# Narrower score matmuls in a dilated attention: 128 key columns in place of 256 for blocks that see one block of keys

## The chip, the cores and the metric

The kernel runs on one core of a Trainium2 chip. The metric is the device time of one execution in microseconds; the time before is the median of three runs. A profile of one further execution gives every instruction's start and duration. The engines are named PE (matmul), PEld (its weight load, which runs beside PE), DVE, ACT, POOL and SP (which issues DMAs).

## The reference

One layer of a decoder: RMSNorm, one input projection, two mixers side by side (a gated linear attention, "GLA", and a dilated sliding-window attention), an output projection, an MLP with squared ReLU, and a final norm. There are 2048 tokens of width 1024, and everything is in float32. The change lies in the dilated attention: 8 heads of width 64, three branches with (window, dilation) of (128, 1), (512, 4) and (2048, 16). In each branch the tokens are sorted by their residue modulo the dilation, and cut into blocks of 128:

```python
qb = to_sub(q).reshape(B, dilation, H, nb, L, Dh)     # L = 128
kb = band(to_sub(k))                                  # a block and the one before it
s = jnp.einsum('bdhcqe,bdhcke->bdhcqk', qb, kb).astype(f32) + bias[:, None]
s = jnp.where(mask, s, NEG)
m = jnp.max(s, axis=-1, keepdims=True)
p = jnp.exp(s - m)
den = jnp.sum(p, axis=-1, keepdims=True)
o = jnp.einsum('bdhcqk,bdhcke->bdhcqe', p, vb.astype(f32)) / den
```

A query block sees its own block of keys and the one before it. The first block of each residue has none before it. With 2048 tokens that is 1 block of 16 for dilation 1, 4 of 16 for dilation 4, and all 16 for dilation 16, where each residue has one block only.

## The kernel before

**Stages.** The kernel has four stages on PE: the input projection (to about 524 us of the profile), the attention together with the GLA (524 to about 862), the output projection, and the two MLP products (to the end). The projections and the MLP are computed as sums of products of the type `float32r` (FR in the code), a float32 whose low mantissa bits are rounded away: each operand is split into a high and a low part, and `mm3` (L141 to L144) adds three products. The attention's scores use the same type: the head dimension of 64 is doubled to 128 rows of the array, high and low parts of the queries against the high part of the keys at L852 (`k1`) and against the low part at L854 (`k2`). Transposes, value products and the GLA are in plain float32.

**Blocks and units.** For each head and branch there are 16 query blocks n. A `Unit` is 2 blocks (branches 0 and 1) or 4 blocks (branch 2). `Unit.scores` takes them in pairs; a pair shares one bank of PSUM (`ps_c`), 256 columns for each block. `windows(br, n)` says from which block of keys on the scores are computed (`first`) and which of the two blocks that follow are used (`used`). A block with two blocks of keys uses both. A block with one is computed for 256 columns too, and half of them are left aside: in branches 0 and 1 the second half, which is the next block; in branch 2 the second half, which is the next residue, but for n = 15, which starts at residue 14 and uses the second half. `k_cols` cuts the 256 columns out of the keys: contiguous in branch 0, with stride 4 in branch 1 (32 x 8 columns of one residue), and 2 x 16 x 8 columns of two neighbouring residues in branch 2.

**What follows the scores.** DVE adds the bias to the used columns and reduces each row (L864), ACT takes the exponential (L865). `Unit.transpose` turns each used 128x128 block on PE (L874) and copies four of them at a time to SBUF (L881 on ACT or L883 on DVE). `Unit.values` multiplies each with 65 columns of values (L893), and DVE takes four blocks from PSUM (L896).

**What sets the order.** The loop at L1186 writes, for each k, the scores of unit k + 3, the transposes of unit k and the values of unit k - 2 alternately, with a step of the GLA (`gla_steps`) after most units, and other work by a plan in units (`at_unit`): packing of queries on POOL (`pack_q`, L806), combining of the branches (`combine`, L921), loads by SP. From L731 on this program order isn't binding: the program is built with `schedule_with_timeline_sim=True`, so a planner with its own prices for instructions places them on the engines' queues, apart from those that the code pins with `keep_in_program_order`. The GLA step has a round trip: L1020 on PE, L1021 on ACT, L1023 and L1026 on POOL, L1033 on PE.

Of the kernel before, what the change touches and what calls it, by code (L numbers as in the profile page):

```python
# [116 lines left out]
def emit(tc, a, stop=99):  # L117
    nc = tc.nc
    V, A, G, T, SP = nc.vector, nc.scalar, nc.gpsimd, nc.tensor, nc.sync
# [6 lines left out]
    def ps(tag):  # L126
        return psum.tile([128, 512], F32, name="ps_" + tag, tag=tag, bufs=BANKS[tag])
# [5 lines left out]
    def view(t, shape):  # L133
        n = int(np.prod(shape))
        names = "abcd"[:len(shape)]
        return t[:, :n].rearrange(f"p ({' '.join(names)}) -> p {' '.join(names)}", **dict(zip(names, shape)))
# [475 lines left out]
    with tc.manual_schedule(engines={nc.tensor.engine, nc.vector.engine, nc.scalar.engine, nc.gpsimd.engine}):  # L612
# [22 lines left out]
        w = view(first_w[0][0], (2, 4, 256))  # L635
# [172 lines left out]
    def windows(br, n):  # L808

        step = (1, 4, 1)[br]  # L810
        if br == 2:
            return (n, [0]) if n < 15 else (n - 1, [1])
        return (n, [0]) if n < step else (n - step, [0, 1])

    def k_cols(t, br, first):
        if br == 0:
            return t[:, 128 * first:128 * first + 256]
        if br == 1:
            b, r = divmod(first, 4)
            return t.rearrange("p (x r i) -> p r x i", r=4, i=8)[:, r, 16 * b:16 * b + 32, :]  # L820
        return t.rearrange("p (x r i) -> p r x i", r=16, i=8)[:, first:first + 2]

    turn = [0]
    ring = {}
# [1 line left out]
    def work(name):  # L826
        i = ring.get(name, 0)
        ring[name] = (i + 1) % 4
        return ring[name + "s"][:, i]

    class Unit:
# [6 lines left out]
        def scores(self):  # L838

            br, h = self.b.br, self.b.h  # L840
            qs, k1, k2 = self.b.head
            qs = packed.get((h, br), qs)
            O = self.b.O
            pe = work("pe")
            each = 2 if br < 2 else 1
            for at in range(0, len(self.ns), 2):
                sp = ps("c")
                rest = []
                for e, n in enumerate(self.ns[at:at + 2]):
                    first, used = windows(br, n)  # L850
                    q, s = qs[:, 128 * n:128 * n + 128], sp[:, 256 * e:256 * e + 256]
                    T.matmul(s, q, k_cols(k1, br, first), start=True, stop=False)  # L852
                    yield
                    T.matmul(s, q, k_cols(k2, br, first), start=False, stop=True)  # L854
                    w = 128 * len(used)
                    s = s[:, 128 * used[0]:128 * used[0] + w]
                    p = pe[:, 128 * each * (at + e):128 * each * (at + e) + w]
                    rest.append((n, s, p, w, used, first))
                    if e == 0:
                        yield  # L860
                for n, s, p, w, used, first in rest:
                    bias = nb[br][:, h, :] if w == 256 or br == 2 else nb[br][:, h, 128:]
                    nm = O[:, n, 130 + h % 2:131 + h % 2]
                    V.tensor_tensor_reduce(p, s, bias, scale=1.0, scalar=BIG, op0=OP.add, op1=OP.min, accum_out=nm)  # L864
                    A.activation(p, p, AF.Exp, bias=nm, scale=-1.0)  # L865
                    for i, u in enumerate(used):
                        self.blocks.append((p[:, 128 * i:128 * i + 128], n,
                                            first + ((1, 4, 1)[br] if br < 2 else 1) * u, u == used[0], u == used[-1]))
                yield
# [283 lines left out]
    for pr in range(4):  # L1153
# [3 lines left out]
        for hh, br in seq:  # L1157
            b = Branch()
            b.h, b.br = 2 * pr + hh, br
            m = 4 if br == 2 else 2  # L1160
            first = len(units)
# [238 lines left out]
    for at, t in enumerate(tiles):  # L1400
# [8 lines left out]
        p = [ps("a"), ps("a")]  # L1409
# [179 lines left out]
    first, parts_at = 7 * (NP - 1), {}  # L1589
# [9 lines left out]
    for at in range(7, len(jobs1)):  # L1599
# [10 lines left out]
        n = at + 6 - len(jobs1)  # L1610
# [15 lines left out]
    for ph, (_, chained, _, _) in enumerate(PRODUCTS):  # L1626
# [3 lines left out]
        for k in range(4):  # L1630
            n = 4 * ph + k
# [74 lines left out]
```

## Time and profile before

| | |
|---|---|
| median of 3 runs | 2267.77 us (2267.43 to 2269.95) |
| the profiled execution | 2271.47 us |
| its span from first to last instruction | 2269.7 us |
| mean granted clock of TensorE | 0.998 |
| L852, L854: matmuls of scores | 384 rows each |
| L874: transposes | 600 rows |
| L893: value products | 1200 rows |

In views of groups a row reads: line, engine, operation, output and inputs, shapes, count, busy time in us, mean ns of one, idle time before them and what ended it. In a timeline a row reads: start and length in us, engine, line, operation, operands, count of merged instructions. In a view by stretches a row reads: the stretch, its length, then busy us and count of each engine, the granted clock, the share of DMA and GB/s. Rows of waits read: who waited for whom, us in total, times, the longest in us. PE's matmuls overlap in the records, so distances between starts say what one costs, and durations do not.

### The profile page before, as it was taken

The page shows a single profiled execution, that of the slowest core. Times are in us where ns is not written, and L with a number is a line of the kernel's source. Part 1 is how long each engine was busy: PE and PEld are TensorE (multiplying, and loading weights), DVE is VectorE, ACT ScalarE, POOL GpSimd, SP SyncE. Part 2 cuts the span into 40 slices and gives each one's busy share as a digit, 9 for nine tenths or more (in the row PEclk, how much of TensorE's full clock was granted, in tenths as well). Part 3 has the DMA queues.
Part 4 walks back from the last instruction along what each step waited for, and adds up shares of the span by engine and source line. Part 5 has one row for each costly group of instructions (what it writes and reads, how often), then busy time and mean ns, then how long its engine had stood idle before and what let it go on. Part 6 is the DMA issues. An engine that isn't in the chain of part 4 may idle for free.

```text
span 2269.7 us, 35245 instructions
## 1 busy us (share of the span) xinstructions
PE 2242.1 (99%) x12508; PEld 1941.8 (86%) x12508; DVE 1632.6 (72%) x3092; ACT 1219.0 (54%) x2421; POOL 481.5 (21%) x455
## 2 busy tenths in 40 slices
PE   9999999999999999999999999999999999999998
PEld 8978998799999998888788887888878888888877
DVE  7788778766667676445867678767776696566798
ACT  6665446535777784324655557555555533333446
POOL 1110002025285673000000000000006322032462
PEclk9999999999999999999999999999999999999999
DMA  5458754787668864678645456454479997677775
GB/s 199 138 175 241 250 166 123 221 249 231 197 210 245 262 199 158 208 229 270 216 128 165 128 165 212 153 177 151 140 241 278 312 320 259 207 249 256 259 257 190
DMA packets 361441, 478.59 MB, mean 211 GB/s; under 512 B 19958, under 2 KB 269319, under 8 KB 350129
## 3 DMA queue, kind: packets, MB, share of 16 engines
q1 hardware_dynamic: 356766, 467.69, 63.7%
q0 software_dynamic: 4352, 8.39, 2.0%
q8 instruction: 98, 1.61, 0.3%
q14 instruction: 79, 0.64, 0.1%
q10 hardware_dynamic: 146, 0.27, 0.0%
HBM read 326.54 MB, written 154.44 MB: 212 GB/s over the span
## 4 chain that ended last, share of the span: by engine, by line
PE 90%; DMA 3%; DVE 2%; issue 2%; POOL 1%; ACT 1%; POOLq 0%; SPq 0%; DVEq 0%; ACTq 0%
PE ps_a L143 10%; PE ps_a L142 10%; PE ps_a L144 10%; PE ps_c L143 8%; PE ps_c L142 8%; PE ps_c L144 8%; PE ps_a L893 4%; PE ps_d L143 4%; PE ps_o L144 4%; PE ps_d L144 4%; PE ps_o L143 4%; PE ps_o L142 4%; PE ps_d L142 4%; PE ps_d L874 3%; PE ps_c L852 2%; PE ps_c L854 2%
## 5 line engine op out<-in xcount | busy, mean ns | idle before, releaser
L1500 POOL TENSOR_TENSOR bs<-bs,rb 128x1024 f32<-128x1024 f32 x60 | 179.1, 2993 | 1069.9 <-DVE ca L487 836.2
L486 ACT ACTIVATE cb<-bs 128x1024 fp32r<-128x1024 f32 x104 | 110.3, 1061 | 287.7 <-issue 144.0
L487 DVE TENSOR_TENSOR cb<-bs,cb 128x1024 fp32r<-128x1024 f32 x104 | 161.1, 1549 | 139.6 <-ACT cb L486 139.6
L487 DVE TENSOR_TENSOR w1comb<-w1raw,w1comb 128x512 fp32r<-128x512 f32 x224 | 153.3, 686 | 90.6 <-ACT w1comb L486 90.0
L865 ACT ACTIVATE pe<-pe,O 128x256 f32<-128x256 f32 (+1 forms) x384 | 156.5, 453 | 45.8 <-DVE O L864 42.3
L893 PE MATMUL ps_a<-v,pt 128*128 128x65 f32 x1200 | 178.5, 253 | 2.5 <-ACT pt L881 1.9
L486 ACT ACTIVATE w1comb<-w1raw 128x512 fp32r<-128x512 f32 x224 | 139.4, 626 | 75.6 <-PE ps_c L144 26.7
L893 PEld LDWEIGHTS ps_a<-v,pt 128*128 128x128 f32 x1200 | 175.3, 195 | 3.5 <-ACT pt L881 2.1
L874 PE MATMUL ps_d<-ident,pe 128*128 128x128 f32 x600 | 159.4, 279 | 0.0
L864 DVE CUSTOM_DVE_ANT_0 pe<-ps_c,nb 128x256 f32<-128x256 f32 (+1 forms) x384 | 126.3, 360 | 40.9 <-PE ps_d L874 18.1
L286 ACT ACTIVATE wcomb<-wraw 128x512 fp32r<-128x512 f32 (+2 forms) x119 | 90.0, 757 | 98.7 <-PE ps_a L143 31.3
L142 PE MATMUL ps_c<-hb,w1comb 128*128 128x512 f32 x336 | 130.8, 389 | 0.5 <-ACT xs L1371 0.5
L143 PE MATMUL ps_c<-hb,w1comb 128*128 128x512 f32 x336 | 130.7, 389 | 0.0
L144 PE MATMUL ps_c<-hb,w1comb 128*128 128x512 f32 x336 | 130.5, 389 | 0.0
L487 DVE TENSOR_TENSOR ca<-ra,ca 128x1024 fp32r<-128x1024 f32 x84 | 121.8, 1451 | 0.1
L144 PE MATMUL ps_c<-cb,ca 128*128 128x512 f32 x312 | 121.4, 389 | 0.0
L143 PE MATMUL ps_c<-cb,ca 128*128 128x512 f32 x312 | 121.4, 389 | 0.0
L142 PE MATMUL ps_c<-cb,ca 128*128 128x512 f32 x312 | 121.4, 389 | 0.0
L1362 ACT ACTIVATE acc<-acc 128x512 f32<-128x512 f32 x96 | 60.7, 632 | 93.8 <-DVE acc L1377 40.4
L874 PEld LDWEIGHTS ps_d<-ident,pe 128*128 128x128 f32 x600 | 110.0, 187 | 0.1
L351 POOL TENSOR_TENSOR acc<-acc,misc 128x264 f32<-128x264 f32 (+1 forms) x32 | 39.2, 1237 | 313.4 <-DVE acc L350 287.0
L142 PE MATMUL ps_a<-wo,mT 128*128 128x512 f32 x256 | 101.3, 396 | 0.0
(411 smaller groups left out, 7111.4 us busy)
## 6 DMA issues: line engine op xcount, KB each, us to landing
ra<-actD SPq DMA_DIRECT2D x52, 1024.0 KB, 7.5
actD<-ring SPq DMA_DIRECT2D x176, 256.0 KB, 2.9
rb<-w_ff SPq DMA_DIRECT2D x88, 512.0 KB, 6.0
bs<-w_ff SPq DMA_DIRECT2D x72, 512.0 KB, 5.6
w1raw<-w_ff SPq DMA_DIRECT2D x64, 512.0 KB, 4.2
k<-kD SPq DMA_DIRECT2D x16, 1024.0 KB, 8.3
wraw<-w_in SPq DMA_DIRECT2D x48, 256.0 KB, 3.4
cmb<-boD SPq DMA_DIRECT2D x16, 528.0 KB, 7.6
```

What stands on the lines that cost most here:

```text
L142: T.matmul(out, sh, mh, start=first, stop=False, **kw)
L143: T.matmul(out, sl, mh, start=False, stop=False, **kw)
L144: T.matmul(out, sh, ml, start=False, stop=last, **kw)
L286: A.activation(hi, src, AF.Copy, scale=sc)
L486: A.activation(hi, src, AF.Copy)
L487: V.tensor_tensor(lo, src, hi.bitcast(F32), op=OP.subtract)
L864: V.tensor_tensor_reduce(p, s, bias, scale=1.0, scalar=BIG, op0=OP.add, op1=OP.min, accum_out=nm)
L865: A.activation(p, p, AF.Exp, bias=nm, scale=-1.0)
L874: T.transpose(pb[:, i * 128:i * 128 + 128], src, ident)
L893: T.matmul(self.b.opsum[:, n % 4], self.pt[:, i * 128:i * 128 + 128], self.b.v[:, blk, cols], start=first, stop=last)
L1362: A.activation(v, v, AF.Relu)
L1500: (engines or ((G,), (V, V))[len(sums) - 1])[e].tensor_tensor(v, v, r, op=OP.add if op == "+" else OP.subtract)
```

## The change

Score matmuls are computed for as many columns as there are blocks of keys in `used`: 128 or 256. In branch 2 `first` is always n and the keys of one residue are taken, 16 x 8 columns. The used part of a block's scores now always begins at the block's first column of PSUM, so the offset by `used[0]` goes away. The reduction, the exponential, the transposes and the value products keep their shapes.

```diff
         step = (1, 4, 1)[br]
         if br == 2:
-            return (n, [0]) if n < 15 else (n - 1, [1])
+            return n, [0]
         return (n, [0]) if n < step else (n - step, [0, 1])
 
-    def k_cols(t, br, first):
+    def k_cols(t, br, first, n):
         if br == 0:
-            return t[:, 128 * first:128 * first + 256]
+            return t[:, 128 * first:128 * first + 128 * n]
         if br == 1:
             b, r = divmod(first, 4)
-            return t.rearrange("p (x r i) -> p r x i", r=4, i=8)[:, r, 16 * b:16 * b + 32, :]
-        return t.rearrange("p (x r i) -> p r x i", r=16, i=8)[:, first:first + 2]
+            return t.rearrange("p (x r i) -> p r x i", r=4, i=8)[:, r, 16 * b:16 * b + 16 * n, :]
+        return t.rearrange("p (x r i) -> p r x i", r=16, i=8)[:, first]
...
                     first, used = windows(br, n)
-                    q, s = qs[:, 128 * n:128 * n + 128], sp[:, 256 * e:256 * e + 256]
-                    T.matmul(s, q, k_cols(k1, br, first), start=True, stop=False)
+                    w = 128 * len(used)
+                    q, s = qs[:, 128 * n:128 * n + 128], sp[:, 256 * e:256 * e + w]
+                    T.matmul(s, q, k_cols(k1, br, first, len(used)), start=True, stop=False)
                     yield
-                    T.matmul(s, q, k_cols(k2, br, first), start=False, stop=True)
-                    w = 128 * len(used)
-                    s = s[:, 128 * used[0]:128 * used[0] + w]
+                    T.matmul(s, q, k_cols(k2, br, first, len(used)), start=False, stop=True)
```

## The prediction

> **What bounds the kernel now.** I read the page first: the busy shares, then the chain that ended last.
>
> ```profile
> span 2269.7 us, 35245 instructions
> ...
> PE 2242.1 (99%) x12508; PEld 1941.8 (86%) x12508; DVE 1632.6 (72%) x3092; ACT 1219.0 (54%) x2421; POOL 481.5 (21%) x455
> ...
> PE 90%; DMA 3%; DVE 2%; issue 2%; POOL 1%; ACT 1%; POOLq 0%; SPq 0%; DVEq 0%; ACTq 0%
> ```
>
> PE is busy for 99% of the span and is 90% of the chain. The change touches two matmul lines, L852 and L854, which run only in the attention stage, from 524 to about 862 us. So the second view is the busy time by stretches of that stage, and the third PE's waits in it.
>
> ```profile
> core 0: us, PE busy (x) PEld busy (x) DVE busy (x) ACT busy (x) POOL busy (x), PEclk, DMA share, GB/s
> ...
> 600.00:700.00 100.00, 100.00 (x894) 98.90 (x894) 68.57 (x307) 77.46 (x234) 57.65 (x83) 1.00 0.70 215
> 700.00:800.00 100.00, 100.00 (x901) 98.90 (x901) 70.45 (x302) 79.44 (x243) 69.26 (x100) 1.00 0.85 263
> ```
>
> ```profile
> PE ps_o L1033 <- POOL gla L1023: 2.0, 1, 2.0
> PE ps_a L893 <- ACT pt L881: 1.9, 1, 1.9
> PE ps_c L852 <- DVE O L864: 0.8, 1, 0.8
> ```
>
> Between 600 and 800 us PE never pauses, and PEld, the weight load, is busy 98.9%. PE waits 4.7 us in the whole stage. ACT is the next engine, with a fifth of its time free. What a matmul takes from PE there is therefore end-to-end time, one for one, up or down. But two things are full, the array and the weight load, so the question is which of them a narrower matmul meets. Matmul durations in the trace overlap, so I use distances between starts.
>
> **How many matmuls change.** The scores of a block with one block of keys go through the 128-column form of the row reduction at L864:
>
> ```profile
> L864 DVE CUSTOM_DVE_ANT_0 pe<-ps_c,nb 128x128 f32<-128x128 f32 x168 | 40.8, 285 | 8.4 <-PE ps_d L874 1.7 <-PE ps_c L854 1.5 <-ACT gla L1064 1.3
> ```
>
> 168 blocks, each with one L852 and one L854, are 336 matmuls. From `windows`: per head 16 blocks of branch 2, 4 of branch 1 and 1 of branch 0; times 8 heads that is 128 + 32 + 8 = 168. So 256 of the matmuls are of branch 2 and 80 of the others.
>
> **What one costs now.** Three stretches in which scores follow scores, in branch 2, 1 and 0 in this order:
>
> ```profile
> 560.48 0.30 PE L852 MATMUL ps_c<-k,qp 128*128 128x256 f32 x1
> 560.61 0.30 PE L854 MATMUL ps_c<-k,qp 128*128 128x256 f32 x1
> ...
> 561.81 0.34 PE L893 MATMUL ps_a<-v,pt 128*128 128x65 f32 x2
> ```
>
> ```profile
> 574.68 0.28 PE L854 MATMUL ps_c<-k,qp 128*128 128x256 f32 x1
> ...
> 575.27 0.28 PE L852 MATMUL ps_c<-k,qp 128*128 128x256 f32 x1
> ```
>
> ```profile
> 594.24 0.28 PE L854 MATMUL ps_c<-k,qs 128*128 128x256 f32 x1
> ...
> 594.83 0.28 PE L852 MATMUL ps_c<-k,qs 128*128 128x256 f32 x1
> ```
>
> Branch 2: 10 starts from 560.48 to 561.81, 1.33 us, 133 ns each. Branches 1 and 0: 5 starts in 0.59 us each, 118 ns. Branch 2 reads keys 16 apart for two neighbouring residues, and pays 15 ns more for the same 256 columns.
>
> **What one costs after: the floor of the weight load.** No matmul of this rounded 4-byte kind (FR in the code) is narrower than 256 columns in the trace, so the price has to be bounded. Each score matmul loads its own 128 columns of weights (the queries), the second of a pair the same ones again. The nearest row for a matmul with little array work and a fresh load is a run of value products:
>
> ```profile
> 870.62 1.00 PE L893 MATMUL ps_a<-v,pt 128*128 128x65 f32 x8
> 871.46 0.49 PE L510 MATMUL ps_d<-ident,mx 128*128 128x128 f32 x3
> ```
>
> Eight records with only 65 columns take 0.84 us, 105 ns each, while the load of each is as large as that of a score. The cheapest mixture is the cycle of one transpose and two value records, where the loads come closest together:
>
> ```profile
> 561.99 0.28 PE L874 MATMUL ps_d<-ident,pe 128*128 128x128 f32 x1
> 562.10 0.33 PE L893 MATMUL ps_a<-v,pt 128*128 128x65 f32 x2
> ...
> 562.56 0.28 PE L874 MATMUL ps_d<-ident,pe 128*128 128x128 f32 x1
> ```
>
> The next transpose is at 562.27 and the one after at 562.56: 0.57 us for two cycles, 285 ns for three loads, 95 ns each. And plain 4-byte products of 128 columns:
>
> ```profile
> 577.99 0.39 PE L1053 MATMUL ps_o<-gla 128*128 128x128 f32 x2
> ...
> 579.33 0.27 PE L874 MATMUL ps_d<-ident,pe 128*128 128x128 f32 x1
> ```
>
> Twelve records (L1053 and L1054 in turn, two each) in 1.34 us: 112 ns each. So a record that loads 128 fresh columns takes 95 to 112 ns whatever it multiplies. I take **110 ns**, near the upper end, since scores mostly follow scores and not the cheap transposes.
>
> The Trainium skill ("TensorE: Matmul & The Clock Gate", section "LDWEIGHTS (loading the stationary operand)") reckons a weight load in ns as its columns divided by 1.2: 106.7 for 128. The 105 and 112 ns above agree with it, and the sum below by that figure would be 7.6 us.
>
> **The sum.** Branch 2: 256 x (133 - 110) = 5.9 us. Branches 1 and 0: 80 x (118 - 110) = 0.6 us. Together 6.5 us less on PE. With 112 it is 5.4 + 0.5 = 5.9 us, with 95 it is 9.7 + 1.8 = 11.5 us. If the narrow form keeps today's distances it is 0.
>
> **What else moves.** Nothing on DVE, ACT or POOL: the reduction, the exponential, the transposes and the value products have the shapes of before. The score block of n = 15 in branch 2 now lies in the first half of its 256 columns of PSUM and not in the second. No DMA and no wait is added; the keys are read in half the columns. Instruction order in this stage is set by a planner with its own prices for matmuls, which may exchange neighbours on PE. That I cost at nothing, because each record is near the floor whatever stands beside it; its bounds are the 4.7 us of waits that it could win and as much that it could add. The POOL chain (combining of branches, then L1026) on which PE waits at the end of the stage starts from PE:
>
> ```profile
> 831.61 1.13 PE L1033 MATMUL ps_o<-gla 128*128 128x256 f32 x4 [2.04 <-POOL gla L1023]
> ```
>
> By then nearly all changed blocks are done, so the chain and the PE work before it move together, and the wait stays 2 us. Cover for ACT: 6.5 us off 338 raises its share from 79% to 81%, so it doesn't become the bound.
>
> The profiled execution was 2271.47 us (span 2269.7 and 1.8 around it), 3.7 above the median of 2267.77. I take the 6 us off the median: **2262 us**, 0.3% less.
>
> **Rivals.**
>
> *The narrow form loses the fast rate (slower).* The fast rate is shown only from 256 columns up; no row says that it holds below. Plain 4-byte products are issued as two records each:
>
> ```profile
> L893 PE MATMUL ps_a<-v,pt 128*128 128x65 f32 x1200 | 178.5, 253 | 2.5 <-ACT pt L881 1.9
> ...
> L874 PE MATMUL ps_d<-ident,pe 128*128 128x128 f32 x600 | 159.4, 279 | 0.0
> ```
>
> (600 blocks of values, 1200 records). If a score matmul below 256 columns runs like those, it costs two records of 112 ns, 224 ns, in place of 133 or 118: 256 x 91 + 80 x 106 = 23.3 + 8.5 = 31.8 us more, 2299.6 us. The mechanism needs only that the width decides the mode, with the point somewhere between 128 and 256 columns. For it: the kinds share 4-byte operands and engine, and the gap in the evidence lies exactly there. Against it: the change alters no type, and a score matmul is one record today. The Trainium skill ("FP8 and Floating Point Precision", section "TensorE Precision Notes") says that true 4-byte products take four passes; the 112 ns records agree with two passes of 128 columns each, and the page is silent on narrow matmuls of the rounded kind.
>
> *The array alone sets the price (faster by more).* 512-column products of the rounded kind:
>
> ```profile
> 877.21 0.39 PE L143 MATMUL ps_a<-wo,mT 128*128 128x512 f32 x1
> ...
> 877.90 0.39 PE L143 MATMUL ps_a<-wo,mT 128*128 128x512 f32 x1
> ```
>
> Three in 0.69 us: 230 ns, against 118 for 256, thus 0.44 ns for a column; 128 columns would take 118 - 56 = 62 ns. Gain: 256 x 71 + 80 x 56 = 18.2 + 4.5 = 22.7 us, 2245 us. It needs loads of the rounded kind to be nearly twice as quick as those of the plain kind; the runs at 105 to 112 ns and PEld at 98.9% speak against it. The Trainium skill ("TensorE: Matmul & The Clock Gate", section "Back-to-back issue gap") gives N/2.4 + 2.5, that is 55.8 ns, for 128 columns, and about 81 ns where each matmul has its load; by 81 the gain would be 16.3 us. The run at 105 ns contradicts it for 4-byte weights.
>
> *Nothing is gained.* Distances stay at 118 to 133 ns because something other than the columns sets them (for branch 2 the load of the packed queries beside the strided keys), or the planner's new order gives the gain back: 2267.8 us. Against it: the difference between 118 and 133 goes with how the keys are read.
>
> **How the numbers follow.** Forecast 0.46, slower form 0.37, array alone 0.06, nothing gained 0.11. Below 0.2%, 4.5 us, this kernel's measurement can't tell a change from none. The forecast's own range, floors of 95 to 115 ns and some planner's noise, is 2255 to 2264; a fifth of it falls within 0.2%. Faster: 0.37 + 0.06 + a little of the last = 0.44; same 0.18; slower 0.38. To leave out no more than two in ten, the range must reach the slower form: 2254 to 2301. It leaves out the array alone and the dearest tenth of the slower form.
>
> **What would show it.** L852 and L854 split into 216 rows of 256 columns and 168 of 128 each. In branch 2, starts of neighbouring scores 105 to 115 ns apart show the floor of the load; about 224 ns, or two records for each narrow matmul, shows the lost rate; 62 the array. The rounds of L893 and L874 keep their 285 ns. I am wrong if the stage's length changes by other than 5 to 12 us, or if PE's waits in it grow past their 4.7 us.

## The result, and the profile after

| | before | after |
|---|---|---|
| median | 2271.62 us (2267.43 to 2274.73, 20 runs) | 2267.11 us (2261.87 to 2269.24, 20 runs) |
| the profiled execution | 2271.47 us | 2268.81 us |
| its span, mean granted clock | 2269.7 us, 0.998 | 2266.9 us, 0.995 |

The ratio is 0.9979, 95% [0.9973, 0.9986]: 0.21% faster, or 4.5 us between the medians. That is at the edge of the 0.2% that the prediction took for the least that can be told from no change; the interval itself excludes no change. The forecast was 2262 us, 0.25% below the median that was known then; that ratio lies inside the interval, but the time misses by 5.1 us.

The page of the changed kernel, in the lines that were read before:

```profile
span 2266.9 us, 35208 instructions
...
PE 2239.0 (99%) x12508; PEld 1937.2 (85%) x12508; DVE 1635.2 (72%) x3092; ACT 1216.7 (54%) x2421; POOL 484.8 (21%) x455
...
PE 90%; DVE 3%; issue 2%; DMA 2%; POOL 1%; ACT 1%; POOLq 0%; SPq 0%; ACTq 0%; DVEq 0%
```

PE still sets the time, with the same 12508 matmuls: no narrow matmul was split into two records. Groups by shape of the changed kernel (L853 and L855 are L852 and L854 of before; every later line has moved up by one):

```profile
L853 PE MATMUL ps_c<-k,qp 128*128 128x128 f32 x160 | 41.9, 292 | 1.3 <-DVE O L863 1.3
...
L853 PE MATMUL ps_c<-k,qs 128*128 128x128 f32 x8 | 2.3, 286 | 0.0
```

160 + 8 = 168 blocks have the narrow form, as counted. What one costs is again read from distances between starts, here in branch 2 where the row before showed 133 ns:

```profile
604.82 0.28 PE L855 MATMUL ps_c<-k,qp 128*128 128x128 f32 x1
604.93 0.28 PE L853 MATMUL ps_c<-k,qp 128*128 128x128 f32 x1
605.04 0.28 PE L855 MATMUL ps_c<-k,qp 128*128 128x128 f32 x1
...
605.93 0.28 PE L855 MATMUL ps_c<-k,qp 128*128 128x128 f32 x1
```

Eleven starts, 1.11 us from the first to the last: 111 ns each. Over all such neighbours in the stage the median is 112.

The stage by stretches, the changed kernel:

```profile
core 0: us, PE busy (x) PEld busy (x) DVE busy (x) ACT busy (x) POOL busy (x), PEclk, DMA share, GB/s
...
600.00:700.00 100.00, 100.00 (x923) 98.81 (x923) 71.11 (x315) 78.95 (x240) 57.71 (x83) 1.00 0.68 214
700.00:800.00 100.00, 100.00 (x917) 98.82 (x916) 68.99 (x296) 81.09 (x251) 72.12 (x105) 1.00 0.84 265
```

In the undisturbed 200 us PE now fits 923 + 917 matmuls where it had 894 + 901: 2.5% more. So the gain is there. But the stage is not shorter by all of it. I summed the start distances of all PE records from the first score to the last value product of the attention, and split them: **PE's work** (a distance over 320 ns, or one at half clock, counts as the median of its kind), the excess in **waits**, and the excess in stretches at **half clock**. A kind is a record's shape together with the next one's. With kinds by the record's own shape alone, work falls by 5.4 us in place of 6.0, so each of these terms is good to some 0.6 us.

| us | stage | PE's work | waits | half clock |
|---|---|---|---|---|
| before | 351.7 | 342.4 | 6.1 | 3.1 |
| after | 348.3 | 336.4 | 8.0 | 3.8 |

Work fell by 6.0 us; the prediction's sum was 6.5, and 5.9 with its upper price of 112 ns. Waits and half clock took 2.6 us back. A second profile of the changed kernel has a stage of 350.6 us, only 1.1 us shorter than before, with more of both (8.7 and 5.9 us). The waits of the changed kernel:

```profile
PE ps_a L892 <- DVE pt L882: 4.3, 2, 4.0
PE ps_c L853 <- DVE O L863: 1.3, 1, 1.3
PE ps_a L892 <- ACT pt L880: 0.9, 2, 0.6
```

The 2.0 us behind L1033 that I took as fixed are no longer among them; a wait of 4.0 us for transposed blocks has come at the end of the stage, and the wait for `O` at 530 us grew from 0.8 to 1.3. That one has a sequel. Stretches around it, of the kernel before:

```profile
529.00:530.20 1.20, 0.42 (x5) 0.22 (x3) 1.20 (x8) 0.94 (x3) 1.20 (x2) 1.00 0.85 212
530.20:532.70 2.50, 2.50 (x21) 2.50 (x22) 2.50 (x18) 2.50 (x10) 2.50 (x5) 1.00 1.12 308
532.70:536.20 3.50, 3.50 (x35) 3.50 (x33) 2.41 (x13) 2.54 (x7) 2.10 (x4) 1.00 1.12 366
```

And of the changed kernel:

```profile
529.40:531.20 1.80, 0.50 (x5) 0.18 (x2) 1.80 (x6) 1.12 (x4) 1.80 (x2) 1.00 0.82 238
531.20:532.70 1.50, 1.50 (x14) 1.50 (x15) 1.50 (x13) 1.50 (x7) 1.50 (x4) 1.00 1.17 307
532.70:536.20 3.50, 3.50 (x20) 3.50 (x19) 2.06 (x13) 2.07 (x8) 3.16 (x5) 0.51 1.13 361
```

PEclk is 0.51 for the 3.5 us behind the longer wait, with 20 matmuls in place of 35, while PE counts as busy throughout. A busy share alone hides this; the number of matmuls and the clock show it. Not all half-clock time of the profiled pair belongs to the change: of the four stretches in the changed kernel's record (the end of the program left out), two, from 184.59 and from 2181.39 us, lie in stages that the change does not touch. The kernel before has two, both in the attention.

### The profile page after: what moved, and what is told of

It reads as the page before. It is cut to its first block, busy times and chain, and to the rows that moved or that the text cites. A ratio compares the mean times of both kernels' runs of the same rounds, so it can differ in the third digit from the quotient of the medians.

```text
span 2266.9 us, 35208 instructions
## 1 busy us (share of the span) xinstructions
PE 2239.0 (99%) x12508; PEld 1937.2 (85%) x12508; DVE 1635.2 (72%) x3092; ACT 1216.7 (54%) x2421; POOL 484.8 (21%) x455
## 4 chain that ended last, share of the span: by engine, by line
PE 90%; DVE 3%; issue 2%; DMA 2%; POOL 1%; ACT 1%; POOLq 0%; SPq 0%; ACTq 0%; DVEq 0%
PE ps_a L143 10%; PE ps_a L142 10%; PE ps_a L144 10%; PE ps_c L143 8%; PE ps_c L142 8%; PE ps_c L144 8%; PE ps_a L892 4%; PE ps_d L143 4%; PE ps_d L142 4%; PE ps_d L144 4%; PE ps_o L144 4%; PE ps_o L142 4%; PE ps_o L143 4%; PE ps_d L873 3%; PE ps_c L855 2%
## 5 line engine op out<-in xcount | busy, mean ns | idle before, releaser
L487 DVE TENSOR_TENSOR cb<-bs,cb 128x1024 fp32r<-128x1024 f32 x104 | 156.4, 1504 | 133.4 <-ACT cb L486 133.3
```

Of the source, the lines that this page charges most:

```text
L487: V.tensor_tensor(lo, src, hi.bitcast(F32), op=OP.subtract)
```

## The experiments

The theory: the price of the narrow scores falls as the prediction reckoned, and what is missing went into PE's order, its waits and the clock. Its rival: the narrow scores themselves gain less than reckoned.

### Program order on PE, both kernels

```diff
-    gla = gla_steps()
-    for k in range(-AHEAD, NU + LAG):
+    with tc.manual_schedule(engines={nc.tensor.engine}):
+        gla = gla_steps()
+        for k in range(-AHEAD, NU + LAG):
...
```

The whole loop of L1186 stands under it, once in the kernel before and once in the changed one; PE then runs its instructions as written, in the same order in both.

> The kernel before, with PE's instructions of the attention loop (L1186 to L1210) kept in the order of the program, so that the planner doesn't move matmuls. It is the base for the next run, which has the same PE order. Weight-load theory and its rivals alike: score distances of 133 ns (branch 2) and 118 ns (others) as before, 768 score matmuls. The total may be above or below before by some tens of us, since the alternating order may wait more; no theory needs a value.

> The changed kernel with the same fixed order on PE as the run before it. Theory (the narrow matmul costs the weight load, 112 ns, and the part of the gain that is missing went into PE waits and stretches at half clock that the planner's new order brought): 5.0 to 6.5 us less than the fixed-order kernel before, with about equal waits and half-clock stretches in both. Rival (the narrow matmul itself saves less than 133 - 112 and 118 - 112 ns in the mixture with transposes and value products): 3 to 4.5 us less here too.

Before: 2312.52 us (2309.69 to 2314.78), ratio 1.0176 [1.016, 1.0192]. Changed: 2303.93 us (2300.02 to 2305.46), ratio 1.0139 [1.0123, 1.0155]. With the order fixed the change is worth 8.6 us between the medians, more than either theory said, though by the two intervals anything from 4 to 14 us. PE's work tells more: in the stage it fell from 366.2 to 355.4 us, 10.8 us, while the rest of the stage, waits and half clock, was 29.6 and 27.0 us. Why is in the timeline. The kernel before in program order, one round:

```profile
600.42 0.27 PE L874 MATMUL ps_d<-ident,pe 128*128 128x128 f32 x1
600.53 0.33 PE L893 MATMUL ps_a<-v,pt 128*128 128x65 f32 x2
600.67 0.36 PE L852 MATMUL ps_c<-k,qs 128*128 128x256 f32 x1
600.87 0.27 PE L874 MATMUL ps_d<-ident,pe 128*128 128x128 f32 x1
```

The changed one, two rounds:

```profile
700.33 0.29 PE L873 MATMUL ps_d<-ident,pe 128*128 128x128 f32 x1
700.46 0.33 PE L892 MATMUL ps_a<-v,pt 128*128 128x65 f32 x2
700.60 0.31 PE L855 MATMUL ps_c<-k,qp 128*128 128x128 f32 x1
700.75 0.29 PE L873 MATMUL ps_d<-ident,pe 128*128 128x128 f32 x1
700.88 0.33 PE L892 MATMUL ps_a<-v,pt 128*128 128x65 f32 x2
701.02 0.32 PE L853 MATMUL ps_c<-k,qp 128*128 128x128 f32 x1
701.17 0.29 PE L873 MATMUL ps_d<-ident,pe 128*128 128x128 f32 x1
```

Rounds of transpose, two value records and a score take 450 ns with a wide score (600.42 to 600.87) and 420 with a narrow one (700.33 to 700.75, 700.75 to 701.17); without a score they take 285, as the prediction read. So a wide score costs 165 ns in such a round, and not the 118 of a run of scores. Over the stage the medians are 455 ns for a round with a wide score and 419 with a narrow one (a few of these take 394 to 400), so a narrow score saves some 36 ns there, against 6 or 21 in a run; the 10.8 us of work over 336 scores are 32 ns each. "Each record is near the floor whatever stands beside it" is refuted for wide scores. The planner, which the code leaves free to do so, puts scores in runs, where the wide ones are cheap: 662 of the 768 scores stand in runs of four or more in the kernel before and 684 in the changed one, against 142 in program order. With it the change has less to win.

### One part of the change alone

Branch 2 narrow, branches 0 and 1 as before:

```diff
-                    w = 128 * len(used)
-                    q, s = qs[:, 128 * n:128 * n + 128], sp[:, 256 * e:256 * e + w]
-                    T.matmul(s, q, k_cols(k1, br, first, len(used)), start=True, stop=False)
+                    w, kn = 128 * len(used), 1 if br == 2 else 2
+                    q, s = qs[:, 128 * n:128 * n + 128], sp[:, 256 * e:256 * e + 128 * kn]
+                    T.matmul(s, q, k_cols(k1, br, first, kn), start=True, stop=False)
...
```

> Only branch 2 narrow (256 matmuls of 128 columns), branches 0 and 1 at 256 columns as before, planner free. Theory: 256 x (133 - 112) = 5.4 us of the gain stay and 80 x 6 = 0.5 us go, so 0.15% to 0.3% below before, within 1.5 us of the changed kernel; distances of 112 in branch 2 and 118 in the others. If the planner's order is what took the missing part, waits and half-clock stretches differ here from the changed kernel's, and the total moves with them by up to 4 us either way.

And the reverse, with `kn = 2 if br == 2 else len(used)` and branch 2's `windows` and keys as before:

> Only the 80 matmuls of branches 0 and 1 with one block of keys are narrow, branch 2 stays at 256 columns; planner free. Weight-load theory: 80 x 6 = 0.5 us less on PE, not measurable. What the total shows beyond that, up to 3 us either way, is what another order of the planner, with other waits and half-clock stretches, does by itself. If narrow matmuls beside transposes and value products save more than in runs of scores (as the two fixed-order kernels suggest, about 60 ns each), up to 4 us less.

Branch 2 alone: 2268.32 us, ratio 0.9982 [0.997, 0.9994]. The others alone: 2268.67 us, ratio 0.9989 [0.9976, 1.0002]. Both intervals are as wide as the whole gain, so these times don't part the two. PE's work in the stage does: 337.7 us with branch 2 alone, 4.7 less than before, and 341.1 us with the others, 1.3 less. Together that is the 6.0 of the whole change. The prediction had 5.9 and 0.6, or 5.4 and 0.5 with 112 ns.

### What sets the floor: 64 columns

```diff
-        return t.rearrange("p (x r i) -> p r x i", r=16, i=8)[:, first]
+        return t.rearrange("p (x r i) -> p r x i", r=16, i=8)[:, first, :8]
...
```

In the changed kernel, branch 2 takes only the first 64 of each block's 128 keys: its scores, bias, reduction and exponential are done on 64 columns. Transposes and value products keep their shapes.

> Branch 2 computes scores for 64 of the 128 key columns (the bias, the reduction and the exponential are over 64 columns as well; the other half of each block is left out), all else as in the changed kernel. Weight-load theory: score distances in branch 2 stay at 110 to 112 ns, and the total is within 0.15% of the changed kernel. Rival (a matmul of this kind below 256 columns runs at half the rate, two steps of the array for each column, which also gives 107 + 5 = 112 ns at 128 columns): about 53 + 5 = 58 ns at 64 columns, and some 256 x 54 = 13 us less. Array-alone rival at one step a column: below 50 ns.

2267.52 us, ratio 0.9982 [0.9972, 0.9992]: nothing gained over 128. Its timeline in branch 2:

```profile
560.32 0.28 PE L853 MATMUL ps_c<-k,qp 128*128 128x64 f32 x1
560.43 0.28 PE L855 MATMUL ps_c<-k,qp 128*128 128x64 f32 x1
560.54 0.28 PE L853 MATMUL ps_c<-k,qp 128*128 128x64 f32 x1
560.65 0.28 PE L855 MATMUL ps_c<-k,qp 128*128 128x64 f32 x1
```

110 ns from start to start (0.33 us for three), and a median of 112 over 207 of them. Half the columns cost the same, where the rivals had 58 and below 50 ns, so the number of columns does not set the price at 128. That the load of 128 columns of weights sets it is argued and not shown: no run has a load of another size, a fixed time for each matmul would fit as well, and PEld's 98.8% doesn't tell, since it was 98.9% before, when the same scores cost 118 to 133 ns.

### Why wide scores of branch 2 cost more: contiguous keys

```diff
-        return t.rearrange("p (x r i) -> p r x i", r=16, i=8)[:, first:first + 2]
+        return t[:, 128 * first:128 * first + 256]
```

In the kernel before, branch 2 multiplies with 256 neighbouring keys in place of those of two residues.

> The kernel before, with 256 contiguous key columns in branch 2 in place of the columns of two residues (other keys than the reference's in that branch). If the stride of the keys makes the wide matmul of branch 2 cost 133 and not 118 ns: distances fall to 118 ns and PE does 256 x 15 = 3.8 us less. If something else does (the packed queries as weights): 133 ns stay, and the total is that of before.

2269.91 us, ratio 0.9986 [0.9977, 0.9995]. Its timeline:

```profile
558.80 0.28 PE L854 MATMUL ps_c<-k,qp 128*128 128x256 f32 x1
...
559.75 0.28 PE L854 MATMUL ps_c<-k,qp 128*128 128x256 f32 x1
```

Eight distances in 0.95 us, 119 ns each, where the strided keys took 133. PE's work fell by 3.4 us to 339.0; 256 x 14 ns is 3.6. So the 15 ns were paid for the way in which the keys of two residues are read (their stride and the step from one residue to the next are not told apart), and more than half of the gain in PE's work is that this read no longer limits.

### Is the late wait to be had back?

If the wait of 4.0 us at the end of the stage is the cost, it should be possible to move. DVE is busy there with splitting output weights (L1093 and L1094 in the changed kernel; ACT rounds, DVE subtracts), so I moved these in three ways. Four units earlier, in the changed kernel and in the one before:

```diff
-        at_unit(NU - 28 + 3 * i + AHEAD, load_wo, 1)
+        at_unit(NU - 32 + 3 * i + AHEAD, load_wo, 1)
```

> The changed kernel with the loads and splits of the output weights (load_wo) planned 4 units earlier. Theory: in the changed kernel PE waits 4.0 us at 858 us for DVE, which stood behind the split of output weights that had landed late, and the clock halves for 6.8 us after it; with the splits earlier that wait shrinks, and the total falls by 2 to 5 us below the changed kernel. Rival: the wait comes from the combining and the last row reductions themselves; then nothing or only noise of 2 us.

> The kernel before with the same earlier loads and splits. If the end of the stage became a bound only with the faster scores: no gain here (within 2 us of before). If the end of the stage binds in both: 2 to 4 us less than before, as in the run before this one.

Changed: 2270.02 us, ratio 0.9992 [0.9983, 1.0]. Before: 2270.4 us, ratio 0.9989 [0.9977, 1.0]. In the changed kernel nothing is won: the interval lies wholly above the change's own 0.9979. Yet its wait for L882 has shrunk, to 0.8 us in all; a wait of 2.6 us for another copy of DVE (L895) stands there, and half clock lasts 10.24 us from 863.43. In the kernel before, the 2.3 us between the medians are not to be told from nothing, by the interval; its profile has no half clock in this stage.

The last two loads four units later, and the last two subtractions on POOL, both in the changed kernel, with that kernel itself once more beside them:

```diff
-        at_unit(NU - 28 + 3 * i + AHEAD, load_wo, 1)
+        at_unit(NU - 28 + 3 * i + 4 * (i > 5) + AHEAD, load_wo, 1)
```

```diff
-            V.tensor_tensor(w[:, 1], raw, w[:, 0].bitcast(F32), op=OP.subtract)
+            (G if c > 5 else V).tensor_tensor(w[:, 1], raw, w[:, 0].bitcast(F32), op=OP.subtract)
```

> The changed kernel once more, beside runs of the kernel before on the same chip. Theory (PE does 6 us less, and part of it goes back because PE's waits now trip the clock more often): the executions of this kernel show a lower mean granted clock than those of the kernel before (0.996 against 0.997), and among executions of equal granted clock the difference is 6 to 8 us, more than the 4 to 5 us of all executions. Rival (the narrow matmuls simply save 4 to 5 us): the same 4 to 5 us among executions of equal clock.

> The changed kernel with the last two loads and splits of the output weights planned 4 units later. If DVE's split of late weights in front of the last row reductions is what makes PE wait at 858 us: that wait of 4.0 us shrinks, the half-clock stretch of 6.8 us after it shrinks to 3.4 or goes, and the total falls by 2 to 4 us below the changed kernel. Rival (the end of the stage is bound by the combining, or the planner's order varies anyway): no gain, within 3 us either way.

> The changed kernel with the low parts of the last two output weights computed on POOL and not on DVE. Same question as the run before it: if DVE's queue at the end of the stage holds PE back, 2 to 4 us less than the changed kernel; if the combining does, which needs POOL too, no gain or a loss of up to 3 us.

The changed kernel: 2266.83 us, 0.9976 [0.9967, 0.9985]. Later loads: 2265.53 us, 0.9977 [0.9967, 0.9987]. On POOL: 2267.53 us, 0.9982 [0.9973, 0.999]. The three are not to be told apart. With later loads the long wait is that of the changed kernel to the digit:

```profile
PE ps_a L892 <- DVE pt L882: 4.3, 2, 4.0
```

With the subtractions on POOL the long one is still there, and longer:

```profile
PE ps_a L892 <- DVE pt L882: 4.8, 2, 4.5
PE ps_a L892 <- ACT pt L880: 1.5, 3, 0.7
PE ps_c L853 <- DVE O L863: 1.3, 1, 1.3
```

The waits of the stage add up to 9.7 us by start distances, not less than the 8.0 and 8.7 of the changed kernel's two profiles, and its half-clock excess is 6.7 against their 3.8 and 5.9. So with the last two subtractions off DVE, PE waits as long for the same copies, and the late splits alone are not the cost. But the run did not leave DVE free, which I had overlooked. POOL and DVE in it, ahead of the wait that ends at 866.58 us:

```profile
857.24 2.37 POOL L1094 TENSOR_TENSOR wo<-woraw,wo 128x1024 fp32r<-128x1024 f32 x1
858.23 1.42 DVE L936 TENSOR_TENSOR small<-small,O 128x8 f32<-128x8 f32 x1
859.57 1.08 DVE L938 TENSOR_TENSOR small<-small,cmb 128x8 f32<-128x8 f32 x1
```

And in the changed kernel, ahead of its wait of 4.0 us and behind it:

```profile
857.09 2.26 POOL L952 TENSOR_TENSOR O<-O,cmb 128x512 f32<-128x512 f32 x1
858.48 0.89 DVE L932 TENSOR_TENSOR small<-small,O 128x8 f32<-128x8 f32 x1
...
862.57 0.16 DVE L938 TENSOR_TENSOR small<-small,cmb 128x8 f32<-128x8 f32 x1
```

L938, a small step of the combining, takes 1.08 us on DVE while POOL works and 0.16 while POOL is idle. In seven profiles (the two kernels, and the five runs of this section) all 122 such operations of DVE (two inputs of 128 x 8) that began with POOL idle took at most 0.17 us; of the 88 that began while POOL worked, 46 took 0.44 to 1.42 us. With the subtractions on POOL, five of them in a row took 5.8 us in place of some 0.8, all ahead of the copy that PE waited for. So in these two profiles DVE's queue does hold PE back at the end of the stage, with the combining in it, as the rival of these expectations had it, slowed beside POOL. How much of the 4.0 us that is stays open: no run takes POOL's work away.

What the repeated runs do show is the clock. Each run records its mean granted clock. In the last set, the kernel before had 0.9968 in the mean of 28 runs, the changed one 0.9959 in 10:

| granted clock | before, mean us (runs) | changed, mean us (runs) | difference |
|---|---|---|---|
| 0.995 | 2273.6 (3) | 2268.4 (3) | 5.2 |
| 0.996 | 2273.1 (8) | 2266.6 (5) | 6.5 |
| 0.997 | 2270.5 (9) | 2264.1 (2) | 6.4 |
| 0.998 | 2270.1 (8) | none | |

At equal clock the change is worth 5.2 to 6.5 us, between the 6 to 8 of the theory and the 4 to 5 of its rival, and near the 6.0 of PE's work; the plain medians of this set differ by 4.7. The clock of the changed kernel is lower by 0.0009, and the kernel before loses 3.0 us from 0.998 to 0.996, thus some 1.4 us for that: 4.7 and 1.4 make 6.1. The groups are small, so this supports the account and doesn't prove its parts.

## Why the prediction was right about the narrow matmul and off in its time

The step that failed is the last one: the 6 us were taken off the median of 3 runs, 2267.77 us, and the kernel before runs in 2271.62. Beside it, the sum put the waits behind a new order on PE at nothing and left out the granted clock, and these two took back part of the gain. In detail:

- **PE bounds the stage; its time is end to end.** Right. ACT rose to 79% and 81% in the two full stretches, near the 81% reckoned, and is not the bound.
- **336 matmuls, 256 + 80.** Right, by the 168 rows of each line.
- **Price after, 110 ns from bounds of 95 and 112.** Right at its upper end: 112. The prediction's sum with 112 is 5.9 us, and PE's work fell by 6.0. That the two agree so well is partly luck: branch 2 gave 4.7 us and not 5.4, the others 1.3 and not 0.5, errors of opposite sign.
- **The floor is not the columns.** Right: 64 columns cost what 128 cost. That it is the weight load was not isolated. The Trainium skill ("TensorE: Matmul & The Clock Gate", section "LDWEIGHTS (loading the stationary operand)") gave 106.7 ns for the load; measured are 112 in the median, 5 ns above it.
- **The 15 ns for the keys of branch 2.** Right: contiguous keys took 119 ns.
- **The slower form, 2299.6 us.** Refuted: one record each, 112 ns. **The array alone, 2245 us.** Refuted by 112 ns where it had 62, and by the 64 columns. **Nothing gained.** Refuted, though narrowly: the interval ends at 0.9986. Its second half was right in part, since waits and clock gave some of the gain back.
- **The planner's order costed at nothing, "because each record is near the floor whatever stands beside it".** The reason failed: a wide score costs 165 ns in a round with transposes and values, and the order decides whether it stands there. Even a run showed it before: its first score, behind a transpose, costs 204 ns in the median of the kernel before and a narrow one 145 in the changed kernel, 59 ns less. The value came out nearly right because the planner keeps most scores in runs in both kernels, which the prediction did not use; that is luck.
- **"The wait stays 2 us."** Failed. That wait went, another of 4.0 us came, and waits in the stage grew by 1.9 us in the profiled pair. This lay within the bound of 4.7 us that I had set and then counted as nothing.
- **The granted clock.** Not in the sum at all: failed by omission. The sum priced PE in nanoseconds at full clock, while a wait of PE can cost a second time through the clock behind it. Waits and clock together took back some 1.3 us of the 5.8 forecast in the medians, 2.6 of 6.0 in the stage of the profiled pair.
- **The 6 us taken off the median of 3 runs.** This is the step that failed most: it made three quarters of the miss. Those three, 2267.43 to 2269.95 us, lie at the low end of what the kernel before does: its 20 runs have 2271.62. Of the 5.1 us between 2262 and 2267.11, 3.85 are this base and 1.3 the gain given back. The profiled execution, 2271.47 us, was the better base, and I had written down its 3.7 us to the median as a remark without weighing it.

By my own test (stage shorter by 5 to 12 us, waits not past 4.7) the prediction was wrong in the stage too: 3.4 us in the profiled pair and 1.1 with the second profile, with rows of waits that sum to 6.5 us. (The 4.7 us were read up to 862 us; to the end of the attention at 876 the kernel before has 5.3.)

## What to carry to other kernels

Where PE is full, price a matmul by the distance between starts in the place where it stands, among its real neighbours, and check by a run with fewer columns whether the columns set it: below the floor, cutting columns gains nothing. A gain of a few us in a kernel of 2270 us is the size of its spread between runs, so base a forecast on many runs, or on the profiled execution and its clock, and read PEclk beside busy shares. Time won on the bounding engine need not all be kept: here its pauses grew, and the clock behind them cost again.

## What the hardware showed that I had not expected

**Half clock comes in pieces of 3.41 us, after pauses much shorter than that.** The changed kernel at the end of the stage:

```profile
858.03 0.28 PE L873 MATMUL ps_d<-ident,pe 128*128 128x128 f32 x1
862.28 0.69 PE L892 MATMUL ps_a<-v,pt 128*128 128x65 f32 x2 [3.97 <-DVE pt L882]
862.76 0.42 PE L873 MATMUL ps_d<-ident,pe 128*128 128x128 f32 x1
```

And the stretch from 860 to 867 us of the same kernel:

```profile
860.00:867.00 7.00, 4.72 (x25) 4.72 (x26) 5.97 (x25) 4.24 (x12) 2.75 (x5) 0.53 0.35 117
```

A transpose lasts 0.42 us there and not 0.28. The record of the clock has half speed from 860.43 for 6.83 us, two pieces, and from 532.75 for one piece; the two beginnings are 327.68 us apart, 96 x 3.413. In the kernel before there is a piece after the waits of 2.0 (L1033) and of 1.9 us (L893), at 832.65 and 863.37, 30.72 or 9 x 3.413 us apart, and none after the wait of 0.8 us. With that both traces agree with a fixed grid of 3.41 us, in which a piece with enough idle PE is followed by one at half clock. How much is enough is not one number. In the kernel before, a wait of 1.74 us lies within one piece of its grid, and in the next piece the clock is full, 1.00 (the second row is of a view by stretches):

```profile
1688.71 0.50 PE L143 MATMUL ps_a<-cb,ca 128*128 128x512 f32 x1 [1.74 <-DVE ca L487]
...
1689.40:1692.80 3.40, 3.40 (x17) 2.77 (x16) 3.40 (x5) 0.00 (x0) 0.00 (x0) 1.00 0.89 295
```

In the 13 traces of this case, from 20 to 2250 us, every stretch at half clock begins within 0.06 us of its own trace's grid, and 8435 pieces of the grids ran at full clock. Of those with less than 1.30 us of idle PE, none was followed by half clock; of the 22 with 1.30 to 1.77 us, 7 were; of those with 1.78 us and more, all 29. The Trainium skill ("TensorE: Matmul & The Clock Gate", section "Part 1: The HAM clock gate (the "warmup" mystery)") names a free-running window of that length and a drop after at least one idle window; here the window from 529.34 to 532.75 was idle for only 1.3 us and the drop came. Where a pause falls on the grid would differ from run to run, which would explain the spread of clocks; that is argued, not shown, and so is what decides between 1.30 and 1.77 us.

**The same matmul has several prices.** 256 columns cost 118 ns in a run, 133 with keys 16 apart, and 165 between value products and a transpose; 128 columns cost 112 in a run and mostly 135 in such a round (420 less 285; 109 in the few of 394).

**A small operation on DVE takes up to nine times as long while POOL works.** 0.16 us with POOL idle, up to 1.42 beside it, as the rows of the late wait show.
